# State-space stage of a two-layer encoder: W1 in blocks of four groups, W2 and T through deeper rings

## The chip, the cores and the metric

The kernel runs on one core of one Trainium2 chip. The metric is device time of one execution in microseconds (us). Four compute engines work side by side, each through its own instruction queue in order: TensorE (PE in the profile; its weight loads are listed apart as PEld), VectorE (DVE), ScalarE (ACT) and GpSimd (POOL). SyncE (SP) only issues transfers, and so does POOL here. An instruction waits for semaphores, and whatever stands behind it on its queue waits too.

## The reference, cut to what matters

Batch 1, 256 tokens, width 2048, float32, two layers. The change lies in the odd layer's mixer, a bidirectional diagonal state-space model: 128 groups of 16 channels, each with a complex state of 64, a forward and a backward scan, their sum, a skip term, GELU, and a gated projection.

```python
def mixer_s5(xn, lam_re, lam_im, log_dt, b_re, b_im, c_re, c_im, d_skip, w_val, w_gate):
    u = xn.reshape(bsz, s_len, S5_GROUPS, S5_GROUP_CH)
    for dr, rev in ((0, False), (1, True)):
        lb_re, lb_im, bb_re, bb_im = disc[dr]
        bu_re = jnp.einsum("sgc,gpc->sgp", us, bb_re)
        bu_im = jnp.einsum("sgc,gpc->sgp", us, bb_im)
        _, _, h_re, h_im = lax.associative_scan(combine, (a_re, a_im, bu_re, bu_im), reverse=rev, axis=0)
        outs.append(jnp.einsum("sgp,gcp->sgc", h_re, cr[dr]) - jnp.einsum("sgp,gcp->sgc", h_im, ci[dr]))
    y = outs[0] + outs[1] + d_skip * xn
    g = jax.nn.gelu(y)
    return (g @ w_val) * jax.nn.sigmoid(g @ w_gate)
```

Before it stand an even layer (convolution and attention) and its feed-forward part. After it come a cross-attention into 256 memory tokens, whose keys and values `memn @ wk` and `memn @ wv` do not depend on the state-space stage, and a last feed-forward part.

## The kernel before, in words

**The filler.** Every dense product streams its weights in tiles of 512 KB (`wtile`, L205 to L212): SP loads `raw` (four buffers), ACT rounds it to `hi`, DVE subtracts to get `lo` (three buffers each), and PE multiplies in split precision. A tile of `lin_xs` (L288) is 12 matmuls of 512 columns, one of `lin_ws` (L251, L254) 8 of 512 columns and 8 of 256. The weight tiles from the first one of `xa_wv` on are numbered in this document: tiles 1 to 32 are `xa_wv` and 33 to 64 `xa_wk`, both of `mem_kv(1)`, the keys and values of the second cross-attention; tiles 65 to 80 are the first column block of `s5_w_val` and `s5_w_gate` (65 to 68 and 69 to 72 need the first half of the state-space result, `gT[0]`, 73 to 80 the second, `gT[1]`); then come 16 tiles for each of the other three column blocks.

**The stage** (`s5`). The residual stream was written to DRAM (`d_x`, L979) and comes back with eight tokens of a block on the free axis (`xc`). `rstd`, one number per token on the partitions, is turned into the layout `rr` by a trip through DRAM (`d_r`, L994 and L997). DVE scales (`xg`, L1001), PE transposes (`ps_u`), and `U` holds the input of 32 group sets (called groups below). For each group PE multiplies `U` with `W1` (`ps_sa`, L1024; the trace has 8 records a group), transposes (`ps_st`, L1031), and `st` is filled. After 16 groups (a half) DVE scans 31 steps of four operations (L1049 to L1052), `hprev` is the shifted copy (L1059, L1060), and for each group PE adds `T` times `U` (L1080) and `W2` times `hprev` (L1083). GELU, a transpose (`ps_g`, L1089) and a split into `gT` end a half.

**Loads of the stage.** POOL issues them in order: `W1` of a group is 512 KB, `W2` 512 KB, `T` 256 KB. `W1` of the first eight groups is loaded early into two slots; all later `W1` and `W2` share a ring of two buffers (`s5w`), `T` has two (`s5t`).

**What sets the order.** A scheduler lays the instructions of all queues out when the program is built: it walks the code in program order and lets independent work move ahead where an instruction would wait. So on PE the stage's small matmuls stand in fixed places among those of the filler tiles. In the code before, both halves stand in front of `mem_kv(1)`.

Of the kernel before, what the change touches and what calls it, by code (L numbers as in the profile page):

```python
# [12 lines left out]
F32 = mybir.dt.float32  # L13
# [3 lines left out]
ALU = mybir.AluOpType  # L17
# [17 lines left out]
class Build:  # L35
# [43 lines left out]
    def setup(self):  # L79
        nc, a, C = self.nc, self.a, self.C  # L80
# [899 lines left out]

    def s5(self):
        nc, a, M, S, R = self.nc, self.a, self.M, self.S, self.R
        w1s = S.tile([128, 4, 4, 256], F32, tag="A0", name="w1s")
        load_w1 = lambda gi, w1: nc.gpsimd.dma_start(w1, self.d_w1[gi].rearrange("p g r d -> p g (r d)"))
        w1s2 = S.tile([128, 4, 4, 256], F32, tag="B2", name="w1s2")
        w1s = [w1s[:, i] for i in range(4)] + [w1s2[:, i] for i in range(4)]
        for gi in range(8):
            load_w1(gi, w1s[gi])
# [21 lines left out]
        ST = []  # L1010
        for hf in range(2):
            st = S.tile([128, 2, 32, 64], F32, tag=f"A{1 - hf}", name="st")
            ST.append(st)
            for g2 in range(8):
                ps = self.pst("ps_sa")
                for i in range(2):
                    gi = hf * 16 + g2 * 2 + i
                    if gi < 8:
                        w1 = w1s[gi]
                    else:  # L1020
                        w1 = M.tile([128, 4, 256], F32, tag="s5w", name="w1", bufs=2)
                        dma = load_w1(gi, w1)
                    for q in range(4):
                        nc.tensor.matmul(ps[q * 32 : q * 32 + 32, i * 256 : i * 256 + 256], lhsT=U[:, gi, q * 32 : q * 32 + 32], rhs=w1[:, q, :], start=True, stop=True, tile_position=(0, q * 32))  # L1024
                sb = M.tile([128, 2, 512], F32, tag="y", name="sb", bufs=2)[:, 0]
                nc.scalar.copy(sb, ps)
# [9 lines left out]
        early = S.tile([128, 4, 2, 4, 128], F32, tag="B2", name="early")  # L1036
        with self.tc.issue_after(dma.ins):
            for gi in range(4):
                nc.gpsimd.dma_start(early[:, gi], self.d_w2[gi])
        gT = []  # L1040
        for hf in range(2):
# [13 lines left out]
            nc.gpsimd.memset(hp[0:64, :, :, 0:1], 0.0)  # L1055
            nc.gpsimd.memset(hp[64:128, :, :, 31:32], 0.0)
            for j in range(2):
                hv = st[:, j].rearrange("p k g -> p g k")
                nc.scalar.copy(hp[0:64, j, :, 1:32], hv[0:64, :, 0:31])  # L1059
                nc.vector.tensor_copy(hp[64:128, j, :, 0:31], hv[64:128, :, 30::-1])  # L1060
            gt = S.tile([128, 2, 2, 4, NTOK], F32R, tag=f"A{1 - hf}", name="gT")
            gT.append(gt)
            for g8 in range(2):
                yt = M.tile([128, 8, 8, 16], F32, tag="y", name="yt", bufs=2)
                for b in range(2):
                    ps = self.pst("ps_y")
                    for i in range(4):
                        gl = g8 * 8 + b * 4 + i
                        gi = hf * 16 + gl
                        if gi < 4:  # L1070
                            w2 = early[:, gi]
                        else:
                            w2 = M.tile([128, 2, 4, 128], F32, tag="s5w", name="w2", bufs=2)
                            nc.gpsimd.dma_start(w2, self.d_w2[gi])
# [135 lines left out]
```

## Time and profile before

| | us |
|---|---|
| median of three runs | 2970.7 (2968.07 to 2972.17) |
| profiled execution | 2974.32 |
| its span, first to last instruction | 2972.2 |
| PE busy in it | 2894.4 |
| DVE busy | 2212.7 |
| ACT busy | 1489.2 |

The stage lies between 1541 us, where PE starts with tile 1, and 2012 us, where the last gate product ends. A view by stretch gives, for each stretch, the busy time of each engine, the clock that TensorE was granted as a share of 2.4 GHz, the mean busy share of the 16 DMA engines, and GB/s. The clock has two levels, 1.2 and 2.4 GHz, so a mean of 0.66 is a stretch with about two thirds of its time at the lower one. Busy time of PE is the union of its matmuls; what is missing to the stretch's length is idle time, and an idle row names what ended it.

### The profile page before, as it was taken

How to read it: one execution, taken by the hardware profiler on the slowest of the kernel's cores; microseconds unless marked ns; L12 is line 12 of the kernel's file. 1: busy time of each engine (PE TensorE's matmuls, PEld its weight loads, DVE VectorE, ACT ScalarE, POOL GpSimd, SP SyncE). 2: the span in 40 equal slices, each digit the busy share in tenths (PEclk: the TensorE clock that was granted, in tenths of full speed). 3: DMA queues.
4: the chain of work that ended last, by engine and by line, in shares of the span. 5: the costliest groups of instructions: out<-in, count | busy, mean ns of one | idle time of the engine just before them, and what ended most of it. 6: DMA issues, size and time to landing. Idle time of an engine off the chain costs nothing.

```text
span 2972.2 us, 44442 instructions
## 1 busy us (share of the span) xinstructions
PE 2894.4 (97%) x16765; PEld 2437.6 (82%) x16765; DVE 2212.7 (74%) x3553; ACT 1489.2 (50%) x1999; POOL 269.1 (9%) x512
## 2 busy tenths in 40 slices
PE   8999998999999999999999997999999999999997
PEld 7887886788888888888886775788888888888886
DVE  7899987877899887889754883556567776467764
ACT  5545554454555543555544543545455555345543
POOL 1100022212210202020020122000000000000000
PEclk9999999999999999999999998999999999999999
DMA  6655588978987788687796887555455555555554
GB/s 218 233 191 170 193 243 261 299 253 286 302 291 237 237 275 278 228 265 224 256 320 196 306 300 264 178 189 177 160 198 185 187 185 192 193 186 190 185 191 148
DMA packets 206439, 674.03 MB, mean 227 GB/s; under 512 B 33600, under 2 KB 36176, under 8 KB 205712
## 3 DMA queue, kind: packets, MB, share of 16 engines
q1 hardware_dynamic: 177840, 593.97, 60.5%
q0 software_dynamic: 28384, 77.23, 8.4%
q8 instruction: 131, 2.15, 0.3%
q14 instruction: 84, 0.69, 0.1%
HBM read 620.34 MB, written 61.08 MB: 229 GB/s over the span
## 4 chain that ended last, share of the span: by engine, by line
PE 84%; DMA 7%; issue 5%; DVE 3%; ACT 1%; POOL 0%; SPq 0%; ACTq 0%; POOLq 0%; DVEq 0%
PE ps_xs L288 33%; PE ps_ws L251 31%; PE ps_ws L254 16%; DMA w<-d_w 2%; DVE lo L212 1%; DMA raw<-xa_wq 1%; ACT hi L210 1%; PE ps_xt L157 1%; DMA tq<-d_t 1%; DMA kvraw<-d_kT 1%; DMA raw<-ab_w_out 1%; PE ps_k L945 1%; DMA d_r<-rstd 0%; DVE w1s L845 0%; PE ps_s L439 0%
## 5 line engine op out<-in xcount | busy, mean ns | idle before, releaser
L212 DVE TENSOR_TENSOR lo<-raw,hi 128x1024 fp32r<-128x1024 f32 x960 | 1172.5, 1222 | 572.4 <-ACT hi L210 569.9
L210 ACT CAST hi<-raw 128x1024 fp32r<-128x1024 f32 x960 | 1008.9, 1051 | 1055.3 <-PE ps_xs L288 493.4
L251 PE MATMUL ps_ws<-x,hi 128*128 128x512 f32 x4352 | 1528.4, 397 | 6.2 <-ACT hi L210 4.0
L254 PE MATMUL ps_ws<-x,lo 128*128 128x256 f32 x4352 | 1202.8, 282 | 0.2 <-DVE lo L212 0.2
L251 PEld LDWEIGHTS ps_ws<-x,hi 128*128 128x128 f32 x4352 | 809.1, 188 | 189.7 <-ACT hi L210 4.4
L254 PEld LDWEIGHTS ps_ws<-x,lo 128*128 128x128 f32 x4352 | 821.4, 189 | 18.0 <-issue 4.1
L288 PE MATMUL ps_xs<-hi,hb 128*128 128x512 f32 x1396 | 432.1, 390 | 0.0
L288 PEld LDWEIGHTS ps_xs<-hi,hb 128*128 128x128 f32 x1396 | 262.0, 188 | 54.1
L288 PE MATMUL ps_xs<-lo,hb 128*128 128x512 f32 x698 | 272.3, 390 | 0.0
L288 PE MATMUL ps_xs<-hi,x 128*128 128x512 f32 x640 | 202.4, 394 | 0.0
L852 POOL DMA_DIRECT2D w1s<-d_pw x256 | 122.4, 486 | 605.0 <-DVE w1s L845 263.6
L288 PE MATMUL ps_xs<-hi,gT 128*128 128x512 f32 x512 | 163.3, 398 | 7.1 <-ACT sgt L1111 6.6
L288 PE MATMUL ps_xs<-hi,oT 128*128 128x512 f32 x512 | 160.8, 392 | 0.8 <-ACT hi L210 0.8
L288 PEld LDWEIGHTS ps_xs<-lo,hb 128*128 128x128 f32 x698 | 131.0, 188 | 27.0
L288 PEld LDWEIGHTS ps_xs<-hi,x 128*128 128x128 f32 x640 | 120.3, 189 | 28.7 <-issue 4.6
L288 PE MATMUL ps_xs<-lo,x 128*128 128x512 f32 x320 | 127.6, 399 | 0.9 <-DVE lo L212 0.9
L288 PEld LDWEIGHTS ps_xs<-hi,gT 128*128 128x128 f32 x512 | 97.4, 191 | 30.9 <-ACT sgt L1111 7.9
L260 ACT COPY z<-ps_ws 128x512 f32<-128x512 f32 x88 | 51.6, 587 | 140.7 <-PE ps_ws L251 140.6
L288 PEld LDWEIGHTS ps_xs<-hi,oT 128*128 128x128 f32 x512 | 96.0, 188 | 20.3 <-ACT hi L210 1.0
L657 ACT ACTIVATE c<-z,fdb,fdw 128x256 f32<-128x256 f32 x176 | 96.2, 594 | 31.9 <-DVE z L652 31.9
L513 DVE SCALAR_TENSOR_TENSOR av<-hpt,cdw,av 128x256 f32<-128x256 f32 x240 | 110.4, 483 | 0.7
L261 DVE TENSOR_TENSOR z<-ps_ws,z 128x512 f32<-128x512 f32 x88 | 60.7, 689 | 56.0 <-ACT z L260 55.9
(285 smaller groups left out, 2652.0 us busy)
## 6 DMA issues: line engine op xcount, KB each, us to landing
raw<-ffn_w_up SPq DMA_DIRECT2D x352, 512.0 KB, 3.9
raw<-ffn_w_down SPq DMA_DIRECT2D x176, 512.0 KB, 4.2
raw<-ab_w_in SPq DMA_DIRECT2D x64, 512.0 KB, 3.9
raw<-xa_wv SPq DMA_DIRECT2D x64, 512.0 KB, 3.5
raw<-xa_wk SPq DMA_DIRECT2D x64, 512.0 KB, 4.8
raw<-xa_wq SPq DMA_DIRECT2D x64, 512.0 KB, 4.2
raw<-xa_wo SPq DMA_DIRECT2D x64, 512.0 KB, 3.6
w<-d_w POOLq DMA_DIRECT2D x52, 512.0 KB, 5.7
```

What stands on the lines that cost most here:

```text
L157: nc.tensor.transpose(ps[:, j * 256 + tb * 128 : j * 256 + tb * 128 + 128], src[tb][:, kk * 128 : kk * 128 + 128], self.ident)
L210: nc.scalar.copy(hi, raw)
L212: ins = nc.vector.tensor_tensor(lo, raw, hi.bitcast(F32), op=ALU.subtract)
L251: both = lambda: nc.tensor.matmul(ps[:, c], lhsT=hi[:, kk, sl], rhs=x2, start=first, stop=last)
L254: nc.tensor.matmul(ps[:, c, 1], lhsT=lo[:, kk, sl], rhs=xh, start=False, stop=False)
L260: self.nc.scalar.copy(out, ps[:, :, 1])
L261: self.nc.vector.tensor_tensor(out, ps[:, :, 0], out, op=ALU.add)
L288: ins = mm()
L513: nc.vector.scalar_tensor_tensor(ac[:, ct, :], hp[:, ct, j : j + NTOK], cdw[:, ct, j : j + 1], ac[:, ct, :], op0=ALU.mult, op1=ALU.add)
L657: nc.scalar.activation(c[:, i], zt[:, i, 1 : NTOK + 1], AF.Identity, bias=fdb[:, ft : ft + 1], scale=w(1))
L852: nc.gpsimd.dma_start(pw[t * 16 : t * 16 + 16], self.d_pw[t, k * 4 : k * 4 + 4].partition_broadcast(16))
L945: nc.tensor.matmul(pk[q * 32 : q * 32 + 32, kk, 0:128], lhsT=bb[:, kk * 4 + q, j, :], rhs=wo[:, j * 512 + q * 128 : j * 512 + q * 128 + 12 ...
```

## The change

`W1`, two blocks in slots, is loaded block by block: four groups in a slot, eight blocks, and block b+2 is loaded after the matmuls of block b (`load_quad`). The small `s5w` ring is gone. `W2` has a ring of four buffers for the first half, and twelve for the second: four in slot B1 and eight in the `x2` tiles that `mem_kv(1)` reads its memory tokens from. `T` has five buffers. `rr` comes from a matmul with a constant selection matrix `sel` and no longer from DRAM. The half is split in two functions, `scan` and `outside`, and `outside(1)` stands behind `mem_kv(1)`. The copy into `hprev` goes in three pieces of the group axis, and its four memsets go from POOL to DVE. After each value product, ACT copies the two results out of PSUM (`keep`), and the gate multiplies the copy.

```diff
+    def keep(self, ps):
+        pc = [self.M.tile([128, 512], F32, tag="s5t", name="pvc", bufs=5) for _ in range(2)]
+        for o, p in zip(pc, ps):
+            self.nc.scalar.copy(o, p)
+        return pc
...
+        def load_quad(b):
+            t = S.tile([128, 4, 4, 256], F32, tag=("A0", "B2", "A0", "B2", "B1", "B2", "B1", "B2")[b], name="w1s")
+            for i in range(4):
+                nc.gpsimd.dma_start(t[:, i], self.d_w1[b * 4 + i].rearrange("p g r d -> p g (r d)"))
+            quads.append(t)
...
-        nc.sync.dma_start(self.d_r.rearrange("b p -> p b"), self.rstd, allow_slow_non_contiguous=True)
         rr = M.tile([128, 8], F32, name="rr")
-        for q in range(4):
-            nc.sync.dma_start(rr[q * 32 : q * 32 + 32], self.d_r.rearrange("b (k t) -> (b k) t", t=8))
+        r8 = M.tile([128, 2, 8], F32, name="r8")
+        ps = self.pst("ps_rr")
+        for tb in range(2):
+            nc.vector.tensor_scalar(r8[:, tb], sel[:, 256:264], self.rstd[:, tb : tb + 1], None, op0=ALU.mult)
+            nc.tensor.matmul(ps[:, 0:8], lhsT=sel[:, tb * 128 : tb * 128 + 128], rhs=r8[:, tb], start=tb == 0, stop=tb == 1)
+        nc.vector.tensor_copy(rr, ps[:, 0:8])
...
+        for b in range(8):
...
+            for i in range(4):
+                gi = b * 4 + i
+                for q in range(4):
+                    nc.tensor.matmul(pss[i // 2][...], lhsT=U[:, gi, q * 32 : q * 32 + 32], rhs=quads[b][:, i, q, :], ...)
+            if b < 6:
+                load_quad(b + 2)
...
-            nc.gpsimd.memset(hp[0:64, :, :, 0:1], 0.0)
+            nc.vector.memset(hp[0:64, :, :, 0:1], 0.0)
+            for g in (slice(0, 16), slice(16, 32), slice(32, 64)):
+                for j in range(2):
+                    hv = st[:, j, :, g].rearrange("p k g -> p g k")
+                    nc.scalar.copy(hp[0:64, j, g, 1:32], hv[0:64, :, 0:31])
+                    nc.vector.tensor_copy(hp[64:128, j, g, 0:31], hv[64:128, :, 30::-1])
...
+            if hf:
+                late = S.tile([128, 4, 1024], F32, tag="B1", name="w2r")
+                more = [S.tile([128, 2, 1024], F32, tag=f"x2{i}", name="w2r") for i in range(4)]
+                slots = [late[:, i] for i in range(4)] + [more[i // 2][:, i % 2] for i in range(8)]
+            else:
+                slots = [ring[:, i] for i in range(4)]
...
-                            w2 = M.tile([128, 2, 4, 128], F32, tag="s5w", name="w2", bufs=2)
-                            nc.gpsimd.dma_start(w2, self.d_w2[gi])
-                        tq = M.tile([128, 512], F32, tag="s5t", name="tq", bufs=2)
+                        w2 = slots[gl % len(slots)].rearrange("p (r q x) -> p r q x", r=2, q=4)
+                        nc.gpsimd.dma_start(w2, self.d_w2[gi])
+                        tq = M.tile([128, 512], F32, tag="s5t", name="tq", bufs=5)
...
+        scan(0)
+        outside(0)
+        scan(1)
         self.mem_kv(1)
+        outside(1)
...
-                pv = self.lin_xs(wv, gx, kts)
+                pc = self.keep(self.lin_xs(wv, gx, kts))
                 pg = self.lin_xs(wg, gx, kts)
...
-                nc.vector.tensor_tensor(sg[:, tb], pv[tb], sg[:, tb], op=ALU.mult)
+                nc.vector.tensor_tensor(sg[:, tb], pc[tb], sg[:, tb], op=ALU.mult)
```

Line numbers of the changed kernel are one less from L94 to L977 and 17 to 29 more inside `s5`. The order of every queue is the same as before outside the stage.

The first place is DVE where the stage begins: `rstd` is the last step of the norm, `lo` the filler's, `xg` the scaled input. Before:

```order
L119 TENSOR_TENSOR rstd<-rsq_i,rsq_t 128x2
L212 TENSOR_TENSOR lo<-raw,hi 128x1024 x5
L1001 SCALAR_TENSOR_TENSOR xg<-xc,rr,gq 128x32x16 x8
L212 TENSOR_TENSOR lo<-raw,hi 128x1024 x2
L1008 COPY U<-ps_u 128x512
```

The same queue in the changed kernel (`r` is the product of `sel` and `rstd`):

```order
L118 TENSOR_TENSOR rstd<-rsq_i,rsq_t 128x2
L1012 TENSOR_SCALAR r_14896<-sel,rstd 128x8 x2
L211 TENSOR_TENSOR lo<-raw,hi 128x1024 x2
L1014 COPY rr<-ps_rr 128x8
L1018 SCALAR_TENSOR_TENSOR xg<-xc,rr,gq 128x32x16 x8
L211 TENSOR_TENSOR lo<-raw,hi 128x1024 x3
L1025 COPY U<-ps_u 128x512 x2
```

The eight `xg` moved ahead of three `lo`: before they stand behind that of tile 10, now behind that of tile 7.

The second place is PE among the `W1` products (numbers after `w` and `x` are buffers; `xs` matmuls are filler). Before, at tile 16:

```order
L288 MATMUL ps_xs<-hi,x_14017 128x512 x2
L1024 MATMUL ps_sa<-w_15032,U 32x256 x3
L1031 MATMUL ps_st<-ident,sb 128x128 x4
L1024 MATMUL ps_sa<-w_15032,U 32x256
L1031 MATMUL ps_st<-ident,sb 128x128 x4
L1024 MATMUL ps_sa<-w_15038,U 32x256 x4
L288 MATMUL ps_xs<-lo,x_14017 128x512
```

Now, at tile 12:

```order
L287 MATMUL ps_xs<-lo,x_13970 128x512
L1048 MATMUL ps_st<-ident,sb 128x128 x8
L1037 MATMUL ps_sa<-w1s,U 32x256 x16
L287 MATMUL ps_xs<-hi,x_13970 128x512 x2
L287 MATMUL ps_xs<-lo,x_13970 128x512
```

Where one or two groups stood between pieces of filler, a block of four stands now.

The third place is POOL at the end of the stage, where it issues `W2` (`w`, now `w2r`) and `T` (`tq`); `fdw` belongs to the last feed-forward part. Before:

```order
L1076 DMA tq<-d_t 128x512
L1074 DMA w_16242<-d_w_91 128x1024
L1076 DMA tq<-d_t 128x512
L1074 DMA w_16258<-d_w_91 128x1024
L1076 DMA tq<-d_t 128x512
L1074 DMA w_16274<-d_w_91 128x1024
L629 DMA fdw<-ffn_dw 128x264
```

Now:

```order
L1097 DMA w2r<-d_w_90 128x1024 x4
L1099 DMA tq<-d_t 128x512 x2
L1097 DMA w2r<-d_w_90 128x1024 x3
L1099 DMA tq<-d_t 128x512
L1097 DMA w2r<-d_w_90 128x1024
L1099 DMA tq<-d_t 128x512
L1097 DMA w2r<-d_w_90 128x1024 x6
L1099 DMA tq<-d_t 128x512
L1097 DMA w2r<-d_w_90 128x1024 x2
L1099 DMA tq<-d_t 128x512 x6
L628 DMA fdw<-ffn_dw 128x264
```

`W2` and `T` alternated up to the last group; now up to six `W2` are issued in a row, and `T` follows in its own pace.

## Rows read from the trace of the kernel before

**Rows 1.** The page's first part: busy us (share of the span) and instructions of each engine

```profile
PE 2894.4 (97%) x16765; PEld 2437.6 (82%) x16765; DVE 2212.7 (74%) x3553; ACT 1489.2 (50%) x1999; POOL 269.1 (9%) x512
```

**Rows 2.** By stretch: length, busy time of each engine (instructions), clock, DMA share, GB/s

```profile
1480.00:1550.00 70.00, 70.00 (x310) 57.98 (x309) 37.98 (x48) 30.68 (x39) 19.58 (x29) 1.00 0.96 331
1550.00:1600.00 50.00, 43.51 (x240) 33.59 (x240) 24.32 (x26) 17.82 (x22) 0.67 (x2) 0.93 0.69 187
1600.00:1705.00 105.00, 104.85 (x640) 75.09 (x641) 75.30 (x153) 57.01 (x64) 15.27 (x29) 1.00 0.81 279
1700.00:1710.00 10.00, 10.00 (x65) 8.23 (x64) 8.94 (x22) 5.34 (x7) 1.20 (x3) 1.00 1.02 412
1705.00:1860.00 155.00, 135.73 (x1283) 104.41 (x1282) 98.04 (x221) 66.72 (x84) 29.78 (x57) 0.94 0.80 281
1720.00:1740.00 20.00, 16.32 (x221) 13.16 (x221) 17.07 (x46) 10.00 (x9) 4.78 (x10) 1.00 0.75 253
1780.00:1800.00 20.00, 16.28 (x135) 12.60 (x133) 16.05 (x34) 13.66 (x15) 2.77 (x6) 0.93 0.63 217
1800.00:1820.00 20.00, 18.95 (x162) 14.43 (x160) 6.61 (x7) 7.05 (x9) 4.66 (x9) 0.99 0.88 312
1820.00:1840.00 20.00, 15.52 (x150) 10.23 (x151) 4.60 (x10) 3.69 (x11) 5.32 (x10) 0.66 0.70 238
1840.00:1860.00 20.00, 13.66 (x152) 8.96 (x151) 4.88 (x8) 5.61 (x11) 2.67 (x5) 1.00 0.78 273
1860.00:2030.00 170.00, 162.18 (x743) 133.94 (x742) 93.26 (x116) 81.47 (x106) 0.00 (x0) 0.99 0.55 183
```

**Rows 3.** PE in order of time: start, length, operation, [idle before <- what ended it]

```profile
1576.18 3.65 PE L1007 MATMUL ps_u<-ident,xg 128*128 128x128 f32 x16 [5.57 <-DVE xg L1001]
...
1590.90 1.93 PE L1024 MATMUL ps_sa<-w1s,U 128*32 128x256 f32 x32
...
1596.83 0.63 PE L1024 MATMUL ps_sa<-w1s,U 128*32 128x256 f32 x4
...
1871.33 0.50 PE L288 MATMUL ps_xs<-hi,gT 128*128 128x512 f32 x1 [1.18 <-ACT sgt L1111]
...
1920.35 0.80 PE L288 MATMUL ps_xs<-hi,gT 128*128 128x512 f32 x1 [4.30 <-ACT sgt L1111]
```

**Rows 4.** The chain of waits at the stage's start: start us, us, what

```profile
1551.83 12.84 DMA d_r<-rstd
...
1566.04 4.48 DMA rr<-d_r
```

**Rows 5.** DMA issues, 1540 to 1575 us: size, median us to landing

```profile
w1s<-d_w POOLq DMA_DIRECT2D x4, 512.0 KB, 9.2
...
xc<-d_x SPq DMA_DIRECT2D x1, 512.0 KB, 10.0
```

**Rows 6.** Groups, 1550 to 1860 us: busy us, mean ns | idle before, what ended it

```profile
L212 DVE TENSOR_TENSOR lo<-raw,hi 128x1024 fp32r<-128x1024 f32 x74 | 90.2, 1222 | 83.6 <-ACT hi L210 83.4
...
L1083 PE MATMUL ps_y<-w,hprev 128*32 128x128 f32 x448 | 20.1, 300 | 13.9 <-DMA w<-d_w 10.2 <-ACT hprev L1059 3.0 <-issue 0.7
L1049 DVE TENSOR_TENSOR m<-A,st 128x128 f32<-128x128 f32 x62 | 18.0, 290 | 1.6
...
L1034 DVE COPY st<-ps_st 64x512 f32<-64x512 f32 x16 | 16.8, 1058 | 3.6 <-PE ps_st L1031 3.4
...
L1059 ACT COPY hprev<-st 64x1984 f32<-64x1984 f32 x4 | 14.6, 3700 | 0.0
...
L1001 DVE SCALAR_TENSOR_TENSOR xg<-xc,rr,gq 128x512 f32<-128x512 f32 x8 | 5.4, 745 | 3.1 <-DMA rr<-d_r 3.1
...
L1083 PE MATMUL ps_y<-early,hprev 128*32 128x128 f32 x64 | 2.7, 276 | 2.3 <-ACT hprev L1059 2.3
```

**Rows 7.** DMA issues, 1705 to 1860 us: size, median us to landing

```profile
w<-d_w POOLq DMA_DIRECT2D x26, 512.0 KB, 5.8
```

**Rows 8.** The chain of waits, 1880 to 1925 us: start us, us, what

```profile
1913.27 4.97 DMA kvraw<-d_kT
```

More of the change, by code (lines that the diff above doesn't have):

```diff
@@ L982, in s5 @@
         nc, a, M, S, R = self.nc, self.a, self.M, self.S, self.R
[L983 to L988, printed above, removed]
         gq = M.tile([128, 512], F32, name="gq")
         nc.gpsimd.dma_start(gq, a["s5_gain"])
+        sel = M.tile([128, 2, 512], F32, tag="y", name="sel", bufs=2)[:, 0, 0:264]
@@ L991, in s5 @@
+        nc.gpsimd.dma_start(sel, a["s5_sel"])
+        quads = []
+        def load_quad(b):
[3 more added lines that the diff above has]
+            quads.append(t)
+        for b in range(2):
+            load_quad(b)
         xc = S.tile([128, 8, 512], F32, tag="A1", name="xc")
-        for q in range(4):
-            nc.sync.dma_start(xc[q * 32 : q * 32 + 32], self.d_x[q].rearrange("(k t) f -> k t f", t=8))
@@ L1010, in s5 @@
         ST = []
[L1011 to L1024, printed above, removed]
+        for b in range(8):
+            hf = b // 4
+            if b % 4 == 0:
+                st = S.tile([128, 2, 32, 64], F32, tag=f"A{1 - hf}", name="st")
+                ST.append(st)
+            pss = [self.pst("ps_sa") for _ in range(2)]
+            for i in range(4):
+                gi = b * 4 + i
+                for q in range(4):
+                    nc.tensor.matmul(pss[i // 2][q * 32 : q * 32 + 32, i % 2 * 256 : i % 2 * 256 + 256], lhsT=U[:, gi, q * 32 : q * 32 + 32], rhs=quads[b][:, i, q, :], start=True, stop=True, tile_position=(0, q * 32))
+            if b < 6:
+                load_quad(b + 2)
+            for h in range(2):
+                g2 = b % 4 * 2 + h
                 sb = M.tile([128, 2, 512], F32, tag="y", name="sb", bufs=2)[:, 0]
-                nc.scalar.copy(sb, ps)
+                nc.scalar.copy(sb, pss[h])
                 p2 = self.pst("ps_st")
@@ L1035, in s5, with scan @@
                 nc.scalar.copy(d4[64:128, :, :, ::-1], s4[64:128])
[L1036 to L1041, printed above, removed]
+        ring = S.tile([128, 4, 1024], F32, tag="B2", name="w2r")
+        gT, hps = [], []
+        def scan(hf):
             st = ST[hf]
@@ L1054, in s5, with outside @@
             hp = S.tile([128, 2, 64, 32], F32, tag=f"B{1 + hf}", name="hprev")
-            nc.gpsimd.memset(hp[0:64, :, :, 0:1], 0.0)
[L1056 to L1060, printed above, removed]
+            nc.vector.memset(hp[0:64, :, :, 0:1], 0.0)
+            nc.vector.memset(hp[64:128, :, :, 31:32], 0.0)
+            for g in (slice(0, 16), slice(16, 32), slice(32, 64)):
[3 more added lines that the diff above has]
+                    nc.vector.tensor_copy(hp[64:128, j, g, 0:31], hv[64:128, :, 30::-1])
+            hps.append(hp)
+        def outside(hf):
+            hp = hps[hf]
             gt = S.tile([128, 2, 2, 4, NTOK], F32R, tag=f"A{1 - hf}", name="gT")
             gT.append(gt)
+            if hf:
[4 more added lines that the diff above has]
+                slots = [ring[:, i] for i in range(4)]
             for g8 in range(2):
@@ L1103, in s5 @@
                 self.lin_xs(wv[4:], gx, kts[8:], ps=pv)
+                pc = self.keep(pv)
                 self.lin_xs(wg[4:], gx, kts[8:], ps=pg)
             else:
[L1106 removed]
+                pc = self.keep(self.lin_xs(wv, gx, kts))
                 pg = self.lin_xs(wg, gx, kts)
@@ L1194, in layout @@
     o["s5_gain"] = c(np.repeat(i["norm_mix_g"][1].reshape(4, 1, 512), 32, 1).reshape(128, 512))
+    sel = np.zeros((128, 264), np.float32)
+    for p in range(128):
+        for tb in range(2):
+            sel[p, tb * 128 + tb * 16 + p // 8 : tb * 128 + 128 : 32] = 1
+        sel[p, 256 + p % 8] = 1
+    o["s5_sel"] = sel
     order = [q * 4 + g8 for g8 in range(4) for q in range(4)]
```

8 lines of the change are left out of this document (3 added, 5 removed).

## The prediction

> **What bounds the kernel now.** I read the page's busy times first: PE works 2894.4 of the span's 2972.2 us [rows 1], so no change that keeps PE's matmuls can give back more than the idle 78 us and what the slow clock costs. Then the view by stretch, because the change touches one stage only. In 1480 to 1550 us PE never rests, and 310 matmuls of 512 columns take 70 us, 0.226 us each [rows 2]; a weight tile is 12 of these, 2.71 us. In the state-space stage the same view shows the holes: 50 - 43.51 = 6.5 us in 1550 to 1600, 3.7 in 1720 to 1740, then 3.7, 1.05, 4.5 and 6.3 us in the four stretches from 1780 to 1860, and 170 - 162.2 = 7.8 us from 1860 to 2030. Together 33.6 us. Between 1600 and 1705 there is none, although all the W1 loads of the small ring fall there: filler hides them.
>
> The clock column adds a second loss. A mean of 0.93 over 50 us is 7 us at 1.2 GHz, which costs half of it, 3.5 us. In 1780 to 1800 it is 2.8 us (cost 1.4), in 1820 to 1840, at 0.66, it is 13.6 us with PE busy 78% (cost 5.3), and from 1860 on 3.4 us (cost 1.7). Together 11.9 us. The first drop stands behind the idle 5.6 us at 1576 [rows 3], the others too stand where PE rested. So what the stage can give back is 33.6 + 11.9 = **45.5 us**, and the forecast is 45.5 less what the changed stage will lose itself. PE's matmuls are the same in both kernels.
>
> **The start: rstd by matmul.** The chain shows the trip of `rstd` through DRAM, 12.84 and 4.48 us [rows 4], and DVE waiting for its end, in the row of `xg` [rows 6]. It goes. What is late next is in the same stretch: the last quarter of `xc`, issued at 1551.0 beside four W1 loads, takes 10.0 us [rows 5], so it lands at 1561.0, and `xg` cannot start sooner. It takes 8 x 0.745 = 6.0 us at most [rows 6]; in a row they took 5.4, until 1566.4. Now the order: `xg` stands ahead of `lo` of tile 8. PE has tile 7 done at 1541.2 + 7 x 2.71 = 1560.2 and then needs that `lo`, which ends 1.22 us after `xg`, at 1567.7. PE therefore stands 7.2 us, where it stood 6.5. I take 7.2 and the same 3.5 us for the clock: **10.7 us lost, nothing gained here**. What the step does buy is position: PE is at tile 7.2 at 1567.7 instead of tile 10.1 at 1576.2, so 2.9 tiles of filler are left for later. That is worth only what they cover later. The small operations (two on DVE, two matmuls, a copy) cost nothing as long as `xc` is the later one; if it landed at once, they would show, about 1 us.
>
> **W1 in blocks.** In the order of the changed kernel, counted along PE, blocks 0 to 7 stand between tiles 10 and 23; before, the groups were spread from tile 13 to tile 42. From the end of block 0 to that of block 7, PE has 13.1 tiles (35.5 us), 7/8 of the W1 products (32 records took 1.93 us [rows 3], so 224 take 13.5) and some 9 us of transposes: 58 us. The loads in it are 12.6 MB of W1 and 6.8 MB of weight tiles, with stores 19.9 MB. The stretch 1600 to 1705 moved 279 GB/s at a busy share of 0.81, which is 344 GB/s when full [rows 2]: 57.8 us. On the mean it just fits. Singly, the tightest is block 5: its slot is free after block 3, and PE meets it 1.6 tiles and a block later, some 7.5 us, against a landing of 9.2 us for four such loads [rows 5]. That is 1.7 us. DVE adds something: over the seven tiles from 20 to 27 it has 7 x 1.22 for `lo`, some 62 scan operations at 0.29 and eight copies at 1.06 [rows 6], 35 us, against 29 of PE; the ring of three `lo` buffers lends two tiles, 5.4 us. I take **4 us**, between 0 (PE rested 0.15 us in all of 1600 to 1705) and 12 (every one of five blocks late by 2.4).
>
> **hprev.** Twice PE waited for ACT's copies, 3.0 and 2.3 us [rows 6]. They still take ACT 2 x 3.7 us in a row per half and hold up the next `hi`; the first piece is only ready sooner. I take 4 us for both halves, between 0 and 7. The memsets on DVE replace two of 0.3 us on POOL and are lost in the rest.
>
> **W2 and T.** Waits for W2 ended 10.2 us of PE's idle time in the second half [rows 6]. With two buffers each load was issued when a group ended and landed 5.8 us later [rows 7]. In the new order 24 of 32 groups are through by tile 67, before 18 were; the last eight stand between tiles 67 and 73. Their W2 goes into `x2` slots that come free during the last four tiles of `mem_kv(1)`. From tile 61 to the last group PE has 11.8 tiles (32 us) and some 12 us of small work, 44 us; 12 W2, 11 T and 12 weight tiles are 16 MB. 1705 to 1860 moved 281 GB/s at 0.80 [rows 2], 351 when full: 45.6 us, plus 5.8 to land, less the 8 us of filler that stands ahead of the first. A hole of about 5 us stays, and 2 for the clock: **7 us**, between 2 (all loads in time) and 20 (the two-buffer pattern again).
>
> **keep.** PE waited 1.18 and 4.30 us for the sigmoids [rows 3], because the value product of the next column block needs a PSUM buffer that the gate still holds. With `pv` copied when it is done, that buffer is free a whole product earlier. The copies (8 x 0.6 us on ACT) stand two tiles ahead of need in the order, so no `hi` is late. At 1915 ACT was also held by a wait for `kvraw` [rows 8]; that stays, and the next `lo` will be about 1.2 us late. Of 7.8 us idle and 1.7 of clock, **1.2 stays** (0 to 4).
>
> **Fewer changes of kind on PE.** Four W1 records alone last 0.63 us, thirty-two 1.93 [rows 3]: a lone small group costs about 0.3 us more than its share. The order has 16 such groups of W1 instead of 24 and 23 of W2 and T instead of 27, twelve fewer: 3.6 us gained.
>
> **The sum.** 45.5 - (10.7 + 4 + 4 + 7 + 1.2) + 3.6 = 22.2 us. Against the profiled execution's 2974.3 that is 2952.1; the median of the runs is 3.6 us lower, 2970.7, so the forecast is 2948.5, **2948 us**.
>
> **Rivals.** *All loads land in time.* For it: PE hardly rested between 1600 and 1705, and in 1700 to 1710 the DMA engines moved 412 GB/s [rows 2], with which 16 MB take 39 us. Against it: landings of 9.2 us when loads crowd [rows 5]. Then W1 costs 0, the tail 2: 31 us gained, 2939. Beside this stands a rule of the Trainium skill, DMA: Bandwidth & Descriptors, section "Anatomy of one DMA — SWDGE (gpsimd) path": a load costs about 2.0 us plus its bytes at 436 GB/s, so, as an estimate from that page, 512 KB would be there after 3.2 us. By that rule neither block 5 nor the tail would wait. The trace does not agree: 5.8 and 9.2 us in the rows. Chance 0.2.
>
> *The tail stays bound by its loads.* The twelve slots are filled only as `mem_kv(1)` ends, when the filler is nearly spent and weight tiles crowd the same DMA engines; for it speaks the busy share of 0.88 at 1800 to 1820 with PE still waiting. Then the tail costs 20 instead of 7: 9 us gained, 2961. Chance 0.19.
>
> *Slower: PE stands before the blocks.* Before, two groups at a time were waited for, with filler between; now PE, in order, can't pass a block whose load is late, and blocks 2, 3, 5, 6 and 7 are loaded only after an earlier block is through. The gaps in the order are 12, 12, 7.5, 9 and 10 us. Landings up to 9 us cost nearly nothing; from about 15 us on they cost 3 + 3 + 7.5 + 6 + 5 = 24.5, which eats the gain. At 18 us (twice the 9.2 in the rows) the cost is 39.5 instead of 4, and the time 2948.5 + 35.5 = 2984. Against it: the mean rate is enough. Chance 0.07.
>
> **How the numbers follow.** The forecast has 0.54, the rivals 0.20, 0.19 and 0.07. A measurement of this kernel can tell about 0.2%, 6 us, from no change. Faster by more: the forecast, the first rival and most of the second (0.12), 0.86. Within it: the rest of the second, 0.07. Slower: 0.07. The range 2932 to 2966 holds the forecast with the bounds of its terms, the first rival, and most of the second; the slow rival stays out.
>
> **What would show it.** PE in order of time: a hole of about 7 us ended by `lo` of tile 8 near 1567, the clock low behind it. No wait for `d_r`. The W1 products done by about 1637 instead of 1701, with PE's holes in 1580 to 1640 a few us in all. The last `ps_g` near 1840 instead of 1858. No `sgt` wait ahead of PE. The prediction would be wrong if PE waits for W1 blocks by tens of us, if `xg` starts well before 1561, or if the last eight groups wait for W2 as before.

## The result, and the profile of the changed kernel

The changed kernel takes 2932.1 us, median of four runs (2929.33 to 2933.14), beside 2971.4 for the kernel before on the same chip: a ratio of 0.9862 with a 95% interval of 0.9848 to 0.9875, 39 us faster. The forecast was 2948, between 2932 and 2966: the direction was right, the gain nearly twice what was forecast, and the time at the lower end of the range (the ratio times the 2970.7 of the table is 2929.7, just below it). The profiled span is 2930.9 us, 41.3 less than before.

The page's first line, to be read against [rows 1]:

```profile
PE 2881.2 (98%) x16769; PEld 2436.5 (83%) x16769; DVE 2213.4 (76%) x3568; ACT 1493.2 (51%) x2015; POOL 268.2 (9%) x509
```

PE is busy 13.2 us less, and idle 49.7 us instead of 77.8, 28.1 less: together the 41.3. The view by stretch, with the columns of [rows 2]:

```profile
1550.00:1600.00 50.00, 47.49 (x293) 35.82 (x291) 26.38 (x30) 22.13 (x27) 6.25 (x12) 0.93 0.83 296
1600.00:1705.00 105.00, 104.59 (x760) 78.07 (x758) 86.59 (x198) 61.66 (x66) 14.70 (x28) 1.00 0.74 269
1705.00:1860.00 155.00, 152.56 (x1259) 125.20 (x1259) 102.51 (x208) 74.64 (x109) 22.78 (x43) 1.00 0.77 286
1780.00:1800.00 20.00, 20.00 (x205) 16.05 (x204) 8.41 (x14) 8.48 (x17) 4.25 (x8) 1.00 1.03 415
1800.00:1820.00 20.00, 20.00 (x235) 15.74 (x233) 7.39 (x8) 6.99 (x9) 1.07 (x2) 1.00 0.58 206
1820.00:1840.00 20.00, 19.55 (x86) 15.70 (x85) 10.98 (x17) 11.62 (x20) 0.00 (x0) 1.00 0.54 180
1860.00:2030.00 170.00, 168.44 (x847) 142.35 (x846) 100.03 (x123) 88.46 (x116) 0.00 (x0) 1.00 0.58 195
```

The stage had 33.6 us of holes; it has 2.51 + 0.41 + 2.44 + 1.56 = 6.9 now. The lower clock is left in the first stretch alone: a mean of 0.93 over 50 us costs 3.5 us, where the stage paid 11.9 in all.

PE in order of time, with the columns of [rows 3], from 1541 to the last `ps_g`; of the larger holes there are only these:

```profile
1560.58 0.50 PE L287 MATMUL ps_xs<-hi,x 128*128 128x512 f32 x1 [0.20 <-ACT hi L209]
1563.39 3.68 PE L1024 MATMUL ps_u<-ident,xg 128*128 128x128 f32 x16 [2.31 <-DVE xg L1018]
1566.72 0.78 PE L287 MATMUL ps_xs<-lo,x 128*128 128x512 f32 x1
...
1770.85 0.39 PE L253 MATMUL ps_ws<-x,lo 128*128 128x256 f32 x1 [1.99 <-DVE lo L211]
...
1819.09 1.03 PE L1112 MATMUL ps_g<-ident,yt 128*128 128x128 f32 x8
```

The kernel before, in the same view: the last W1 product and the last `ps_g`. Below them the last W1 product of the changed kernel:

```profile
1701.14 0.64 PE L1024 MATMUL ps_sa<-w,U 128*32 128x256 f32 x8
...
1857.52 1.10 PE L1089 MATMUL ps_g<-ident,yt 128*128 128x128 f32 x8 [0.72 <-ACT yt L1084]
```

```profile
1640.39 0.64 PE L1037 MATMUL ps_sa<-w1s,U 128*32 128x256 f32 x8
```

The last `ps_g` is 38 us sooner now, and 21 us sooner than the 1840 that was foretold. The groups of the stage, to be read against [rows 6] (busy us, mean ns | idle before, what ended it), show that PE never waited for a load of W1, W2 or T:

```profile
L1106 PE MATMUL ps_y<-w2r,hprev 128*32 128x128 f32 x512 | 20.6, 275 | 0.0
L1037 PE MATMUL ps_sa<-w1s,U 128*32 128x256 f32 x256 | 19.2, 387 | 0.0
L1103 PE MATMUL ps_y<-tq,U 128*32 128x128 f32 x256 | 14.1, 276 | 0.0
```

And yet the loads did not land sooner than before. DMA issues from 1705 to 1860 us, to be read against [rows 7] (size, median us to landing):

```profile
w2r<-d_w POOLq DMA_DIRECT2D x22, 512.0 KB, 7.5
...
tq<-d_t POOLq DMA_DIRECT2D x21, 256.0 KB, 6.7
```

A W2 took 5.8 us before and takes 7.5 now. What changed is how early it is asked for.

### The profile page after: what moved, and what is told of

It is laid out like the page before. It is cut to its first block, busy times and chain, and to the rows that moved or that the text cites. A ratio compares the mean times of both kernels' runs of the same rounds, so it can differ in the third digit from the quotient of the medians.

```text
span 2930.9 us, 44468 instructions
## 1 busy us (share of the span) xinstructions
PE 2881.2 (98%) x16769; PEld 2436.5 (83%) x16769; DVE 2213.4 (76%) x3568; ACT 1493.2 (51%) x2015; POOL 268.2 (9%) x509
```

## The experiments

Theory A was that three things act together: W1's blocks bring the scans forward and so leave filler to stand between the W2 groups; the deeper rings let W2 and T be asked for ahead; the early copy ends the waits of the gate products. The rivals give the whole gain to one of these, or to none. All ratios are to the kernel before, run beside them. Three ratios of the changed kernel itself, 0.9862, 0.9877 and 0.9865, have a mean of 0.9868; most intervals reach 0.0015 to either side, 4.5 us, so that an effect of 3 us shows in a profile but is not told apart by the time.

The changed kernel itself, beside the three that follow:

> The changed kernel once more, as the measure for the three beside it: 2932 us, 39 below the kernel before, by every theory.

Measured 2934.75, ratio 0.9877 (0.9863 to 0.9891).

**The early copy, alone and undone.** `e1_keep` is the kernel before with

```diff
+                pv = self.keep(pv)
...
-                pv = self.lin_xs(wv, gx, kts)
+                pv = self.keep(self.lin_xs(wv, gx, kts))
```

> The kernel before with one part of the change alone: the two results of each value product are copied out of PSUM by ACT, and the gate multiplies the copy. Theory A (the parts add up; the gate products lost 7.8 us of idle time and 1.7 of clock, and the copy frees the PSUM buffer that they waited for): 8 us less than the kernel before, 2963; no wait for sgt ahead of PE after 1860, PE idle there below 2.5 us. Rival B (the copy queues on ACT behind the hi of the filler and the wait for kvraw, so PE waits for the copy instead of the sigmoid): 0 to 3 us less, 2968 to 2971, with an idle row ended by pvc.

`e2_no_keep` is the changed kernel with `pc = pv`:

> The changed kernel without the early copy of the value results; all else as in it. Theory A: the two waits for sgt come back, idle 5.5 to 7.8 us plus 1.7 of clock: 2938 to 2941, 6 to 9 above the changed kernel. Rival B (the waits for sgt came from the late end of the stage before, with ACT behind; now ACT is ahead and the sigmoids are there in time): 0 to 2 above, 2932 to 2934.

Alone: 2965.4, ratio 0.9972 (0.9963 to 0.9982), 6 to 8 us. Undone: 2941.4, ratio 0.9898 (0.9884 to 0.9912), 6 above the changed kernel beside it. Theory A by both. With the copy alone PE is idle 1.6 us from 1860 to 2030, where it was 7.8, and no wait for `sgt` is left there. In the profile without the copy, PE in order of time has the old waits again, those of [rows 3]:

```profile
1887.33 0.80 PE L287 MATMUL ps_xs<-hi,gT 128*128 128x512 f32 x1 [4.96 <-ACT sgt L1140]
...
1981.15 0.50 PE L250 MATMUL ps_ws<-x,hi 128*128 128x512 f32 x1 [1.17 <-ACT sgt L1140]
```

**rstd through DRAM.** `e3_dram_rr`:

```diff
-        for tb in range(2):
-            nc.vector.tensor_scalar(r8[:, tb], sel[:, 256:264], self.rstd[:, tb : tb + 1], ...)
-            nc.tensor.matmul(ps[:, 0:8], lhsT=sel[...], rhs=r8[:, tb], ...)
-        nc.vector.tensor_copy(rr, ps[:, 0:8])
+        nc.sync.dma_start(self.d_r.rearrange("b p -> p b"), self.rstd, ...)
+        for q in range(4):
+            nc.sync.dma_start(rr[q * 32 : q * 32 + 32], self.d_r.rearrange(...))
```

> The changed kernel with rstd taken through DRAM again; the order puts ps_u at tile 10.1 again instead of 7.2 and the W1 blocks 0.7 tiles later, the tail as in the changed kernel. Theory A (at the start PE loses what it lost in the kernel before, 6.5 idle and 3.5 of clock, instead of 2.5 and 3.4; the 2.9 tiles of filler that are spent there are not needed later, because the W2 and T loads are far enough ahead): 4 us more than the changed kernel, 2936. Rival B (the earlier position is what feeds the tail, and its loss comes back as idle time of W1 blocks and the tail): 8 us of filler missing, 10 to 12 more, 2942 to 2944, with PE idle in front of ps_sa or ps_y.

Measured 2937.2, ratio 0.9887 (0.9872 to 0.9902): 2.5 to 3 us above, near theory A's 4, and not to be told from nothing. The chain at its start has the store to `d_r` again, 13.45 us, and PE's wait before `ps_u` is 4.07 us, against 2.31 to 2.96 in the changed kernel. The 10 us of rival B are out: PE waits for no W1 and no W2 and 0.6 us for a T, so the 2.9 tiles of filler that are spent early are hardly missed later.

**The rings.** `e4_t2` and `e5_w2four`, which ran beside the two after them:

```diff
-  tq = M.tile([128, 512], F32, tag="s5t", name="tq", bufs=5)
+  tq = M.tile([128, 512], F32, tag="s5t", name="tq", bufs=2)
```

> The changed kernel with two T buffers instead of five (the copies of the value results get two of their own). In the order the last ps_g stands at tile 76 instead of 74: more filler is used up between the last groups. Theory A (depth of the rings is what took PE's waits away; a T load takes 6.7 us to land, and with two buffers it is issued when the group before the last ends): idle rows of ps_y ended by tq, 5 to 10 us in all with the clock behind them, 2940 to 2945. Rival B (the filler between the groups covers the T loads, which are half as large as those of W2; only the order moves): 0 to 2 us above the changed kernel, 2933 to 2937.

```diff
-                more = [S.tile([128, 2, 1024], F32, tag=f"x2{i}", name="w2r") for i in range(4)]
-                slots = [late[:, i] for i in range(4)] + [more[i // 2][:, i % 2] for i in range(8)]
+                slots = [late[:, i] for i in range(4)]
```

> The changed kernel with four W2 slots in the second half instead of twelve (slot B1 alone). The order on PE has the last eight groups in the same tiles, 67 to 73. Theory A (the twelve slots let the last loads go out from 1767 on, 20 us ahead of their groups; with four the last eight wait for groups to end, and a landing of 7.5 us is met twice): 5 to 10 us of idle time ended by w2r between 1785 and 1825 and up to 4 of clock, 2939 to 2946. Rival B (a lead of four groups, some 13 us with the filler between them, covers a landing of 7.5 us): 0 to 2 above the changed kernel, 2933 to 2936.

T with two buffers: 2939.2, ratio 0.9887 (0.9869 to 0.9905), some 5 us above: theory A, though with 3.5 us of waits for T where 5 to 10 were expected, and at the edge of what the intervals tell apart. W2 with four slots in the second half: 2934.7, ratio 0.9867 (0.9849 to 0.9885), nothing: rival B. So the eight slots in `x2` carry no time. The lines of the group views, the first from the kernel with two T buffers, the second from that with four W2 slots:

```profile
L1103 PE MATMUL ps_y<-tq,U 128*32 128x128 f32 x256 | 13.7, 286 | 3.5 <-DMA tq<-d_t 3.5
```

```profile
L1105 PE MATMUL ps_y<-w2r,hprev 128*32 128x128 f32 x512 | 20.7, 276 | 0.0
```

With four slots, loads of 7.2 us that go out only as groups end are still in time.

**The place of the second half.** `e6_w2four_first` is `e5_w2four` with

```diff
-        self.mem_kv(1)
         outside(1)
+        self.mem_kv(1)
```

> As e5_w2four, and the W2 and T products of the second half stand ahead of mem_kv(1) in the program again, as in the kernel before. The last ps_g stands at tile 73.1 instead of 74. Theory A (the place in the program matters only because the scheduler then spends the filler as early as it can, and here it puts the groups at nearly the same tiles): within 3 us of e5_w2four. Rival B (standing behind mem_kv(1) is what keeps filler for the tail): 8 us or more above e5_w2four, with PE idle before ps_y.

Measured 2933.2, ratio 0.9864 (0.9845 to 0.9882), 1.5 us below `e5_w2four`: theory A. The place in the program serves only to make the `x2` slots possible, and these carry no time.

**W1 through a small ring again.** `e7_w1ring`, held against `e4_t2`, since both have two T buffers:

```diff
+                if b < 2:
+                    w1 = quads[b][:, i]
+                else:
+                    w1 = M.tile([128, 4, 256], F32, tag="s5w", name="w1", bufs=2)
+                    nc.gpsimd.dma_start(w1, self.d_w1[gi].rearrange("p g r d -> p g (r d)"))
...
-            if b < 6:
-                load_quad(b + 2)
```

> The changed kernel with the W1 of blocks 2 to 7 through a ring of two buffers again, group by group as in the kernel before, and T in two; rstd, hprev, W2 rings and early copy as changed. It is to be held against e4_t2. In the order the last W1 product stands at tile 40.9 instead of 22.9, the first W2 product at 46.9 instead of 39.9, the last ps_g at tile 76 in both. Theory A (early W1 blocks move their 12.6 MB ahead of the W2 and T loads, and the products of the first half ahead of the tail; without that the last half meets its loads with little filler): 10 to 20 us above e4_t2, idle rows ended by w2r, tq or scan results after 1760. Rival B (the gain sits in the W2 and T rings, the hprev pieces and the early copy, and W1 was covered before too): 0 to 4 above e4_t2.

Measured 2956.5, ratio 0.9944 (0.9928 to 0.9961): 17 us above `e4_t2`, theory A, and the largest single part. Its group lines show where the 17 us turn up:

```profile
L287 PE MATMUL ps_xs<-lo,gT 128*128 128x512 f32 x64 | 26.1, 408 | 4.7 <-DVE lo L211 4.7
...
L1043 PE MATMUL ps_sa<-w,U 128*32 128x256 f32 x192 | 16.5, 390 | 3.3 <-DMA w<-d_w 3.2
L1107 PE MATMUL ps_y<-tq,U 128*32 128x128 f32 x256 | 14.7, 298 | 8.6 <-DMA tq<-d_t 8.5
```

Only 3.3 us stand at W1 itself. The waits for T grow from 3.5 to 8.5 us, a `lo` that stands behind the second half's `hprev` on DVE costs 4.7, and from 1790 to 1830 the clock falls to a mean of 0.83. This kernel's first W2 product stands at tile 46.9 and that of `e4_t2` at 39.9, with the last group at tile 76 in both: the same groups with seven tiles (19 us) less filler among them. It is not that the loads land later there: from 1705 to 1860 W2 takes 8.3 us in the median and T 5.4, in `e4_t2` 8.4 and 4.8. W1's blocks pay at the end of the stage, not where they are.

**hprev whole, and W2 with two slots.** `e9_hprev_whole`:

```diff
-            for g in (slice(0, 16), slice(16, 32), slice(32, 64)):
+            for g in (slice(0, 64),):
```

> The changed kernel with the copies into hprev whole again, 2 of 3.7 us on ACT in a half instead of 6 of 1.1 and 2.0. In the order the first W2 products of each half stand 0.2 to 1 tile later. Theory A (the pieces give PE its first groups sooner; before it waited 5.3 us for ACT's copies): 3 to 5 us above the changed kernel, with idle rows of ps_y ended by hprev. Rival B (the filler ahead of the first group covers the copies in either form; only ACT's total counts, which holds the hi and so the lo): 0 to 1 above.

Measured 2939.4, ratio 0.9888 (0.9875 to 0.9902), 6 us above the mean of the changed kernel: theory A. Its group line has the wait, 2.2 us in the first half and 1.6 in the second:

```profile
L1106 PE MATMUL ps_y<-w2r,hprev 128*32 128x128 f32 x512 | 22.3, 285 | 3.8 <-ACT hprev L1075 3.8
```

`e10_w2two` takes two slots of each ring instead of four and twelve:

```diff
-                slots = [late[:, i] for i in range(4)] + [more[i // 2][:, i % 2] for i in range(8)]
+                slots = [late[:, i] for i in range(2)]
             else:
-                slots = [ring[:, i] for i in range(4)]
+                slots = [ring[:, i] for i in range(2)]
```

> The changed kernel with two W2 slots in both halves, as many as the kernel before; W1 in blocks, five T buffers and all else as changed. In the order the W2 groups go in twos and threes with filler between, and the last ps_g stands at tile 76 instead of 74. Theory A (what feeds the tail is the filler that the early W1 blocks leave for it, 17 us by e7_w1ring; with it between the groups two buffers nearly do, as two for T did): 3 to 6 us above the changed kernel, 2936 to 2940. Rival B (the ring for W2 carries the gain of some 10 us that the early copy, rstd, T and W1 leave unexplained): 9 to 13 above, 2943 to 2947, with 10 us of idle time ended by w2r after 1690.

Measured 2944.2, ratio 0.9912 (0.9896 to 0.9928): 13 us above by the ratios, 10 by the medians, so rival B by the time. Its DMA issues and its group line:

```profile
w2r<-d_w POOLq DMA_DIRECT2D x26, 512.0 KB, 5.9
```

```profile
L1105 PE MATMUL ps_y<-w2r,hprev 128*32 128x128 f32 x512 | 21.3, 282 | 5.6 <-DMA w2r<-d_w 5.6
```

The loads land faster than in the changed kernel, 5.9 against 7.5 us, and PE waits for them 5.6 us, where it waited for none. Of these 4.8 fall between 1812 and 1834, where the DMA engines are busy 0.73 of the time, so they were not full. The wait is a matter of lead, that is of the time between asking for a load and needing it, and not of landing. From 1600 to 1860 PE is idle 9.95 us, against 2.85 with twelve or with four slots in the second half; with the clock (0.96 from 1820 to 1860, a cost of 1.6) this makes some 9 of the 10 to 13 us. So going from two slots to four is worth about 10 us, and from four to twelve in the second half nothing. The figure includes the order, since with two slots the last group stands two tiles later.

The parts do not add up. Taken out one at a time they cost about 6 us (the early copy), 3 (`rstd`), 6 (the pieces of `hprev`), 10 to 13 (the slots of W2), 5 (the buffers of T) and 17 (the blocks of W1, with two T buffers): together more than the 39 gained. Each was measured with the other parts in place, so these costs overlap. None comes to 39, so the rivals that put the whole gain down to one part are out.

**The start.** What the changed kernel still loses ahead of `ps_u` was tried in five ways. `e8_direct` takes the last quarter of `xc` straight from X:

```diff
-        for q in range(4):
+        for q in range(3):
             self.nc.sync.dma_start(xc[q * 32 : q * 32 + 32], self.d_x[q].rearrange(...))
+        for tb in range(2):
+            self.nc.sync.dma_start(xc[96 + tb * 16 : 112 + tb * 16], self.X[:, tb, 1536:2048])
```

> The changed kernel, but the last quarter of xc is copied straight from X in SBUF, and no longer written to d_x and read back. Theory A (xg waits for the last quarter, whose way is a store of 6.3 us and then a load of 8.8; one transfer of some 8 us, issued at 1541, lands before rr is ready at 1554, so xg and ps_u come 3 us sooner and PE's 2.3 to 3.0 us of idle time and the clock of 1 to 3.4 behind it go): 3 to 5 us below the changed kernel, 2928 to 2931. Rival B (PE then waits for a hi of the filler, whose raw crowds the same transfers, and loses the same there): 0 to 1 below.

`f1_direct_first` adds to it what `e6_w2four_first` has:

> e6_w2four_first and e8_direct together: four W2 slots in the second half, its W2 and T products ahead of mem_kv(1) in the program, and the last quarter of xc straight from X. Theory A (the two idle places left in the stage are apart: 2 to 3 us before ps_u, 2.0 before a ps_ws that waits for lo behind the hprev copies, which e6_w2four_first did not have): 1 to 2 us below e8_direct, 2926 to 2930. Rival B (what PE gains at the one place it waits at the other): the same as e8_direct.

Measured 2930.1, ratio 0.9858 (0.9844 to 0.9873), and 2930.4, ratio 0.9859 (0.9844 to 0.9874): 3 us below the changed kernel, inside the spread. In the profile of `e8_direct` the whole stage begins 5.4 us earlier (its four W1 loads go out at 1535.5 instead of 1540.9). Counted from there, `xg` comes 1.6 us later than in the changed kernel, not 3 us sooner, and PE's idle time at the start is 2.3 us instead of 2.5, now in front of a `hi`, a `lo` and `ps_u`: the mechanism is that of rival B. DVE in order of time:

```profile
1552.84 1.23 DVE L211 TENSOR_TENSOR lo<-raw,hi 128x1024 fp32r<-128x1024 f32 x1 [7.12 <-ACT hi L209]
1553.98 0.16 DVE L1016 COPY rr<-ps_rr 128x8 f32<-128x8 f32 x1
1554.18 5.39 DVE L1020 SCALAR_TENSOR_TENSOR xg<-xc,rr,gq 128x512 f32<-128x512 f32 x8
```

`xg` does not wait for `xc` any more. It waits for `rr`, this stands behind a `lo`, and that waits for a `hi` whose `raw` took 14.0 us to land. The filler's own loads had taken the place of `xc`. Is it the 2 MB of W1, issued in the same microseconds, that crowds them? `g3_w1late` (on the changed kernel) and `g2_direct_w1late` (on `e8_direct`) were meant to test that: they hold block 0 until `xc` is there. `f3_all` has both and the order of `f1_direct_first`; the changed kernel ran beside them:

```diff
+            if b == 0:
+                nc.gpsimd.tensor_copy(t[:, :, 0, 0:8], xc[:, 0:4, 0:8])
             for i in range(4):
                 nc.gpsimd.dma_start(t[:, i], self.d_w1[b * 4 + i]...)
```

> The changed kernel beside the three others: 2932 to 2935 us.

> The changed kernel, with the loads of W1 block 0 held until xc has landed (POOL first copies a few elements of xc into the block's slot); the blocks after it move 0 to 1 tile back. Theory A (2 MB less in the DMA engines from 1541 on: xc lands in 6 to 7 us instead of 8.8 and raw in 4.5, so xg starts 2 us sooner and no hi is late; block 0 itself lands some 8 us after 1555, before its products at 1577): 2 to 5 us below the changed kernel, 2928 to 2932, PE idle less than 1 us before ps_u. Rival B (xc is made of small packets and takes as long alone; then nothing is gained at xg, and block 0 comes late instead): 0 to 4 above, 2933 to 2938, with an idle row of ps_sa ended by w1s.

> e8_direct and g3_w1late together. Theory A (in e8_direct the DMA engines were full from 1541 to 1550 and a raw took 14.0 us; without the 2 MB of block 0 that raw is there in 8, rr in time and PE does not rest before ps_u): 4 to 6 us below the changed kernel, 2927 to 2930, and 2 below e8_direct. Rival B (the copy from X alone fills the engines with small packets): as e8_direct, 2930, with PE idle 1.5 to 2.5 us between 1548 and 1562.

> f1_direct_first and g3_w1late together: four W2 slots in the second half, its products ahead of mem_kv(1) in the program, the last quarter of xc straight from X, block 0 of W1 behind xc. Theory A (start and hprev are apart): 2 us below g2_direct_w1late, 2925 to 2928. Rival B (block 0 late moves the blocks back, and the filler that this costs is missing at the end of the half): 0 to 2 above g2_direct_w1late.

Measured: 2933.6 (0.9865), then 2931.3 (0.9857, 0.9843 to 0.9872), 2933.5 (0.9859, 0.9843 to 0.9875) and 2929.0 (0.9847, 0.9833 to 0.9862). But holding block 0 leaves those 2 MB where they are. POOL in order of time, the loads of the first two blocks in the changed kernel, then in `g3_w1late`:

```profile
1474.30 2.11 POOL L1001 DMA_DIRECT2D w1s<-d_w  x4 [70.94 <-PE ps_k L948]
...
1540.90 2.18 POOL L1001 DMA_DIRECT2D w1s<-d_w  x4 [26.56 <-PE ps_xs L287]
```

```profile
1539.04 2.19 POOL L1003 DMA_DIRECT2D w1s<-d_w  x4 [37.16 <-PE ps_xs L287]
...
1556.97 2.08 POOL L1003 DMA_DIRECT2D w1s<-d_w  x4 [0.30 <-POOL w1s L1001]
```

Block 0 was loaded at 1474, into slot A0, long before the stage. What goes out at 1541 is block 1, into slot B2, and it still does so in the three kernels that hold block 0. So neither theory was tested: `xc` took 8.7 us in `g3_w1late`, as before, with the same 2 MB beside it. In `g2_direct_w1late` the `raw` took 13.3 us, and `rr` stood behind its `lo` as in `e8_direct`. Its DMA issues at the start, and PE's row ahead of `ps_u`:

```profile
raw<-xa_wv SPq DMA_DIRECT2D x12, 512.0 KB, 4.6
...
xc<-X SPq DMA_DIRECT2D x2, 256.0 KB, 10.9
```

```profile
1564.62 2.48 PE L1028 MATMUL ps_u<-ident,xg 128*128 128x128 f32 x16 [2.26 <-DVE xg L1022]
```

What delays that `raw` stays open. The two transfers of the quarter stand just ahead of it on SP's queue; whether it waits for them there, for the engines that they keep busy, or for block 1 no run separates. Each of these kernels has PE idle for 2 to 4 us in all at `ps_u` and just ahead of it, ended by `xg`, `hi` or `lo`. `f3_all` has the lowest median of all, 4.6 us below the changed kernel beside it, but the intervals overlap: it beats the kernel before, and that it beats the changed one is not shown.

## Why the prediction was right or wrong, point by point

The frame held: the stage's 33.6 us of holes and 11.9 of clock were what there was to gain, and nothing outside them mattered. It foretold a loss of 26.9 us inside the changed stage; the profile has 10.4: 2.5 and 3.5 at the start, none at W1, 2.4 behind `hprev`, 0.45 after the tail, 1.56 from 1860 on. 45.5 - 10.4 + 3.6 = 38.7, beside 39 by the medians. The miss of 16.5 us is all in the five terms.

**The tail (7 foretold, 0.45 measured), the largest miss.** The step that failed is the balance of bytes and time from tile 61 to the last group. By its own figures it closed: 45.6 us to move, 5.8 to land, 8 of filler ahead make 43.4 against 44. The 5 us of hole stood on no row, and 2 us of clock were put on top. (Of the 10.2 us of waits for W2 that it put in the second half of the kernel before, 1.1 fell in the first, at 1739.) POOL in order of time, the changed kernel: the first and the last row of the twelve W2 that fall into that window.

```profile
1767.29 1.58 POOL L1097 DMA_DIRECT2D w2r<-d_w  x3 [7.78 <-PE ps_ws L250]
...
1781.68 1.04 POOL L1097 DMA_DIRECT2D w2r<-d_w  x2
```

And the same stretch, from tile 61 to the last group, in the view by stretch, with the DMA issues in it:

```profile
1766.90:1816.00 49.10, 47.11 (x532) 37.90 (x532) 21.33 (x26) 20.30 (x29) 11.11 (x21) 1.00 0.87 335
```

```profile
w2r<-d_w POOLq DMA_DIRECT2D x12, 512.0 KB, 10.7
```

The bytes were right: 335 GB/s in 49.1 us are 16.4 MB, where 16 were counted. The window was 49 us and not 44, and the engines moved 335 / 0.87 = 385 GB/s when full and not 351, so the 16.4 MB fill 43 of the 49 us. A W2 takes 10.7 us here in the median, with twelve issued within 15.4 us, and it does not matter: they are asked for by 1782.7, and the last groups run at 1814 to 1816. With four slots the loads go out later and nobody waits either (`e5_w2four`); with two PE waits. So what decides here is not the bytes in the window, but whether the loads are asked for in time.

**The start (10.7 foretold; 6.0 measured).** The step that failed is the order: I had PE need the `lo` of tile 8 before `ps_u`. The row of `ps_u` above is followed by that `lo` at 1566.72; only a `hi` of tile 8 stands ahead. So PE waited for `xg` alone, 2.31 us (2.96 and 2.95 in two other profiles, with up to 2.4 for a late `hi`), and DVE made the `lo` while `ps_u` ran, 3.68 us. Also `xc` was issued at 1549.0 instead of 1551.0 and landed after 8.8 us instead of 10.0, so `xg` began at 1557.9, not 1561, which the forecast had named as a sign that it was wrong (1.0 us of this is that the whole stage begins earlier in this profile). That the clock's 3.5 us came as foretold is partly luck: in one of two other profiles the clock of this stretch is 0.97, a cost of 1.5. Hole and clock together are 6.0, 4.8 and 8.8 us in the three. "Nothing gained here" was wrong by a few us, and `e3_dram_rr` gives 2.5 to 3 to this part; the 2.9 tiles of position, whose worth the forecast left open, are worth nothing that a run shows.

**W1 (4 foretold, none measured).** The mean rate was right: the last W1 product was at 1640.4, where 1637 was foretold, and PE never waited for a block, though the landing was 8.7 us in the median. Block 5, the tightest, was asked for at 1607.8 and met at 1615.8, a lead of 8.0 us, where 7.5 was foretold. The step that failed is the addition of single shortages: by the forecast's own figures 1.7 us for block 5 and 0.6 for DVE (35 less 29 less 5.4), which it rounded up to 4. The larger error is one of place: the forecast gave W1 no gain at all. `e7_w1ring` gives it 17 us, most of it in the waits for T and `lo` at the end.

**hprev (4 foretold, 2.4 measured).** The mechanism was right: ACT's copies hold up the next `hi`. Only the size was off. The row of PE at 1770.85 names a `lo`; on DVE that `lo` waits for a `hi`, and on ACT this `hi` stands behind the six pieces of `hprev`. ACT, then DVE, in order of time:

```profile
1760.72 7.87 ACT L1075 COPY hprev<-st 64x496 f32<-64x496 f32 x6 [1.82 <-DVE st L1067]
1768.50 1.04 ACT L209 CAST hi<-raw 128x1024 fp32r<-128x1024 f32 x1
```

```profile
1769.57 1.22 DVE L211 TENSOR_TENSOR lo<-raw,hi 128x1024 fp32r<-128x1024 f32 x1 [3.53 <-ACT hi L209]
```

The other 0.41 us, the whole idle time from 1600 to 1705, is a wait for `lo` at 1700.5, behind the copies of the first half (ACT, 7.90 us from 1685.9), and is counted here. The pieces take ACT as long as the whole copies, 7.9 us against 2 of 3.7, but the first group no longer waits for them. `e9_hprev_whole` puts the pieces at 6 us by the time, where the forecast let them give back 1.3; its rows show some 4 of these, 2.2 more of idle time from 1600 to 1860 and a clock of 0.98 from 1600 to 1705, a cost of 2.1.

**keep (1.2 to stay; 1.56 stayed).** Right, in the mechanism too: 0.57 and 0.64 us are waits for `lo` at 1885.5 and 1889.9, among ACT's waits for `kvraw` (3.8 us before 1882 and 2.4 before 1891), and the other 0.36 is the wait of a transpose for its input `X`. The gain of 8.3 in the sum is 6 to 8 us by two runs.

**Fewer changes of kind (3.6).** PE's busy time fell by 13.2 us, of which the clock explains 11.9 - 3.5 = 8.4. The 4.8 that are left fit the 3.6; no run shows them apart.

**The rivals.** "All loads land in time" is what PE saw at W1 and in the tail, and with the start sized right it would have given 2934. Of what was put for it, the rate held, 415 GB/s from 1780 to 1800; but the loads did not land faster, they were asked for earlier. The rule that stood beside it, that of the Trainium skill, DMA: Bandwidth & Descriptors, section "Anatomy of one DMA — SWDGE (gpsimd) path", would have 512 KB there after an estimated 3.2 us; the rows have 7.5 in the changed kernel, which does not wait, and 5.9 in `e10_w2two`, which does. So the trace agrees with the result of that rule and not with its figure. The slow rival, PE in front of the blocks, did not occur: the loads landed in 8.7 us and would have needed 15.

## What to carry to other kernels

The waits of PE for loads were cured here by asking for them earlier, not by shorter landings: count how many groups lie between issue and use, and stop adding slots when that lead passes the landing time (here two slots wait, four don't, and twelve in the second half add nothing). Read what a stage costs at its end as well as in its place: finishing W1 60 us sooner removed some 3 us of waits in its place and most of the 17 us 130 to 200 us later, where the order has seven tiles more of filler between the groups. When a forecast balances bytes against a window, a shortage that the figures do not show should not be added by hand; and whether an operand stands ahead of the waiting instruction is to be read from the order, row by row. A wait is followed back over two engines where it has to be: the row of PE named a `lo`, and the cause stood on ACT.

## What was not expected of the hardware

Copying 512 KB from SBUF to SBUF as two transfers took 10.9 us each in the median (10.5 to 11.8 in three other kernels), longer than the load of 512 KB from DRAM in its place, 8.8 us; and a `raw` load issued behind them on the same queue took 13.3 to 14.4 us, where 4.6 is the median of its kind in `g2_direct_w1late`. Two holes of PE of nearly the same length went different ways with the clock. After the 2.31 us at 1563 the granted clock was 0.51 of 2.4 GHz from 1562.6 to 1569.5:

```profile
1562.60:1569.50 6.90, 6.11 (x23) 5.54 (x24) 5.34 (x7) 1.17 (x2) 0.00 (x0) 0.51 0.54 160
```

After the 1.99 us at 1770.85 it stayed at 1.00. What tells the two apart no run shows.
